# Sums of weights in a Strassen-form up-projection: two of four made by an adding transfer, the others by VectorE

## The chip, the cores and the metric

The kernel runs on one core of one Trainium2 chip. The metric is the device time of one execution in microseconds (us), as the median of several runs.

## The reference

The kernel computes two layers of a decoder trunk, for one sequence of 512 tokens and a model width of 1024, in float32. Each layer is a half-step feed-forward network (FFN), a token mixer with three branches, and a second FFN, each conditioned on a vector c. The FFN is where the change lies:

```python
def swiglu(h, w_up, w_down):
    gate, up = jnp.split(h @ w_up, 2, axis=-1)
    return (jax.nn.silu(gate) * up) @ w_down

def reference(x, c, ...):
    for l in range(DEPTH):
        mod = (jnp.einsum('bd,de->be', jax.nn.silu(c), w_ada[l]) + b_ada[l]).reshape(b, 9, d)
        h = modulate(rmsnorm(x, norm_g[l, 0]), mod[:, 0], mod[:, 1])
        x = x + 0.5 * mod[:, 2][:, None] * swiglu(h, w_ffn_in[l, 0], w_ffn_out[l, 0])
        ...
        x = x + mod[:, 5][:, None] * y
        h = modulate(rmsnorm(x, norm_g[l, 2]), mod[:, 6], mod[:, 7])
        x = x + 0.5 * mod[:, 8][:, None] * swiglu(h, w_ffn_in[l, 1], w_ffn_out[l, 1])
    return x
```

D_FF is 2816, so `h @ w_up` is a product of 512x1024 by 1024x5632.

## The kernel before

The six sub-layers are called by their number n from 1 to 6: n = 1, 3, 4 and 6 are FFNs, n = 2 and 5 the mixers. Every float32 operand is split into a high and a low part of type float32r, and every product is three matmuls (high by high, high by low, low by high). For a block of weights `weight` (L254) hands out the pair, `halves` (L219) makes it: ScalarE copies the block into the high part (`wh`, L224), VectorE subtracts that from the block for the low part (`wl`, L228). Blocks are prepared two ahead of their use (`AHEAD = 2`).

Most of the up-projection is done in a form of Strassen's method with seven products where eight would be needed, and four sums on either side. The activations are cut in four quarters (tiles `hq`) and `sums` (L544) makes the four sums of them once at the start of each such stage and splits each (`sh` on ScalarE, `sl` on VectorE at L267). The weights come in pairs of column blocks j; each pair has four quarter blocks 11, 21, 12, 22 of 128x1024 (512 KB). `block` (L231) loads the four on SyncE's DMA queue (SP) into tiles `wr` and makes four sums on VectorE: t1 = 12 - 11 (L244, into a tile `t`), t2 = 22 - t1 (L246, a second tile `t`), 22 - 12 in place of 12 (L248), and 21 - t2 in place of 21 (L251). The products of a pair run in the order 1, 2, 6, 7, 5, then 1 of the next pair, 3, 4; product 1 takes block 11, 2 takes 21, 6 takes t2, 7 takes 22 - 12, 5 takes t1, 3 takes 22 and 4 takes 21 - t2. Each product is 24 matmuls of 128x128 by 128x256 (L582). There are 39 such pairs: 9 in n = 1 and 10 in each of n = 3, 4 and 6. `pair` (L585) adds the products' banks up (L607, L613) and makes silu(gate) * up; columns outside the pairs go through `finish` (L641).

Buffers and queues order the work around this. Raw blocks rotate through 5 buffers, `wh` and `wl` through 3 each. The tiles `t`, the quarters `hq` and the rows `ada` of the conditioning (loads of 512 KB at L428, used by VectorE at L429) share one tag `z` of 4 buffers (`z4k`, L119), so at a stage's start a tile of one kind gets its buffer when a quarter has been read for the last time, by its `sl` split. A scheduler fixes each engine's order of instructions when the program is built. SP issues in its order and waits at an instruction whose buffer isn't free. Conditioning work goes on beside n = 1, 3 and 4, not beside n = 6.

Of the kernel before, what the change touches and what calls it, by code (L numbers as in the profile page):

```python
# [17 lines left out]
ALU = mybir.AluOpType  # L18
# [55 lines left out]
class Trunk:  # L74
# [156 lines left out]
    def block(self, l, f, j, p):  # L231


        sub = self.nc.vector.tensor_tensor
        if p == 1:
            self.pairs[j] = {}
            for q in (11, 21, 12, 22):
                t = self.raw()
                self.nc.sync.dma_start(t, self.io["w_up"][l, f, j, (11, 21, 12, 22).index(q)])
                self.pairs[j][q] = t  # L240
        b = self.pairs[j]
        if p == 6:
            b["t1"] = self.z4k("t")
            sub(b["t1"], b[12], b[11], op=ALU.subtract)  # L244
            b["t2"] = self.z4k("t")
            sub(b["t2"], b[22], b["t1"], op=ALU.subtract)  # L246
        elif p == 7:
            sub(b[12], b[22], b[12], op=ALU.subtract)  # L248
        elif p == 4:

            sub(b[21], b[21], b["t2"], op=ALU.subtract)  # L251
        return b[{1: 11, 2: 21, 6: "t2", 7: 12, 5: "t1", 3: 22, 4: 21}[p]]

    def weight(self, *key):  # L254
        while len(self.loaded) < AHEAD:
# [176 lines left out]
    def ada_done(self, l, s, kind, ks=(0, KD)):  # L432
        nc = self.nc
        a, b = ks
        m0 = (3 * s + kind) * 8
        m = self.mod[l][:, m0 + a:m0 + b]
        o = slice(8 * s + a, 8 * s + b)
        bias = self.p(l, PO_BADA + m0 + a, b - a)
        if kind == 0:
            nc.vector.tensor_tensor(self.shift[l][:, o], m, bias, op=ALU.add)  # L440
        elif kind == 1:
            nc.vector.tensor_tensor(m, m, bias, op=ALU.add)
            nc.vector.scalar_tensor_tensor(self.amp[l][:, o], m, 1.0,
                                           self.p(l, PO_NORM + 8 * s + a, b - a),
                                           op0=ALU.add, op1=ALU.mult)
        else:
            nc.vector.tensor_tensor(self.res[l][:, o], m, bias, op=ALU.add)
            if s != 1:
                nc.vector.tensor_scalar(self.res[l][:, o], self.res[l][:, o], 0.5, None, op0=ALU.mult)

    def ada_jobs(self, l, kinds):
        jobs = []
# [91 lines left out]
    def sums(self):  # L544

        tt = self.nc.vector.tensor_tensor
        a11, a12, a21, a22 = (self.quarters[q] for q in (11, 12, 21, 22))
        self.S = {}

        def keep(n, t):  # L550
            self.S[n] = (self.t4k([P, D], F32R, "sh"), self.t4k([P, D], F32R, "sl"))
            self.split(self.S[n], t)

        tt(a22, a21, a22, op=ALU.add)
        tt(a21, a11, a21, op=ALU.subtract)
        tt(a11, a22, a11, op=ALU.subtract)
        keep(2, a11)
        keep(3, a21)
        keep(1, a22)
        tt(a12, a12, a11, op=ALU.subtract)  # L560
        keep(4, a12)
        self.quarters = {}

# [19 lines left out]
                                     stop=(k, x) == (3, 2), skip_group_check=True)  # L583

    def pair(self, l, f, j, st, nxt, acts):  # L585


        nc = self.nc
        tt = nc.vector.tensor_tensor

        def run(st, j, p, tag, first=True):
            if first:
                st[p] = self.bank(tag)
            self.product(l, f, j, p, st[p], first)

        def snap(name):
            st[name] = self.t2k(name)
            nc.scalar.activation(st[name], st[1], AF.Copy)  # L598

        def more(p):  # L600
            self.product(l, f, j, p, st[1], False)

        if 1 not in st:
            run(st, j, 1, "mm")
        snap("c11")
        run(st, j, 2, "s")
        tt(st["c11"], st["c11"], st[2], op=ALU.add)  # L607
        more(6)
        snap("u2")
        run(st, j, 7, "s")  # L610
        more(5)
        snap("c22")
        tt(st["c22"], st["c22"], st[7], op=ALU.add)  # L613
        later = {}
        if nxt is not None:
            run(later, nxt, 1, "mm")
        more(3)
        self.product(l, f, j, 4, st[7], False)
        act = self.t4k([P, 2, T], F32, "act")
        halves = [act[:, :, h] for h in HALF]  # L620

        def two(t):
            return t.rearrange("p (a b) -> p a b", a=2)

        nc.scalar.activation(st["c11"], st["c11"], AF.Silu)
        tt(halves[0], two(st["c11"]), two(st[1]), op=ALU.mult)
        tt(st["u2"], st["u2"], st[7], op=ALU.add)
        nc.scalar.activation(st["u2"], st["u2"], AF.Silu)
        tt(halves[1], two(st["u2"]), two(st["c22"]), op=ALU.mult)
        hi, lo = self.act_tiles("a")  # L630
        self.split((hi, lo), act)
        for i in range(2):
            acts[2 * j + i] = (hi[:, i, :], lo[:, i, :])
        return later

    def ffn(self, n, l, f, ada, cb, stats, nxt, first=None):
        nc, io = self.nc, self.io
        s = 2 * f
        acts = {}

        def finish(m, pg, pu):  # L641
            sl = self.t2k("sil")
            nc.scalar.activation(sl, pg, AF.Silu)
            nc.vector.tensor_tensor(sl, sl, pu, op=ALU.mult)
            acts[m] = self.act_pair("a")
            self.split(acts[m], sl)

        def unit(g):
            return lambda d: self.weight("down", l, f, g, d)

        def more(k):
            for _ in range(k):
                if ada:
                    ada.popleft()(cb)

        if first:
            banks = [self.bank(t) for t in ("mm", "mm", "mm", "mm", "s", "s")]
            for k in range(KD):
                w = first(k)
                for j in range(6):  # L660
                    self.mm(banks[j], w, slice(j * P, (j + 1) * P), self.h[k], k == 0, k == KD - 1)
            for m in range(3):
                finish(m, banks[2 * m], banks[2 * m + 1])
            self.sums()
            self.ready = True
        early = []
        blocks = self.ffn_blocks(n)
        st = {}
        for (kind, i), after in zip(blocks, blocks[1:] + [("end", 0)]):
            if kind == "plain":  # L670
                if i == 0:
                    early = self.head(lambda j: self.weight("in", l, f, j // 2, j % 2))
                    self.sums()
                ps = []
                for j in range(2):
                    if early:
                        ps.append(early.pop(0))
                        continue
                    w = self.weight("in", l, f, i, j)
                    ps.append(self.bank("mm"))  # L680
                    self.mmk(ps[j], w, self.h, range(KD), 0, KD - 1)
                finish(i, ps[0], ps[1])
                more(2)
            elif kind == "pair":
                st = self.pair(l, f, i, st, after[1] if after[0] == "pair" else None, acts)
                more(2)
            else:
                a, b = GROUPS[i]
                for d in range(KD):
                    w = unit(i)(d)  # L690
                    ps = self.bank("mm")
                    self.mmk(ps, w, acts, range(a, b), a, b - 1, base=a)
                    self.residual(l, s, d, ps, FULL, None)
                    more(2)
        more(len(ada or ()))
        self.tail(l, s, unit(2), acts, GROUPS[2], GROUPS[2][0], stats, nxt)
# [529 lines left out]
```

## Time and profile before

| | |
|---|---|
| median of 3 runs | 2660.65 us (2656.46, 2660.65, 2661.26) |
| profiled execution, its own time | 2660.07 us |
| its span | 2658.3 us |
| TensorE (PE) busy | 2519.4 us, 95% of the span |
| VectorE (DVE) busy | 2005.5 us, 75% |
| ScalarE (ACT) busy | 1126.6 us, 42% |
| GpSimd (POOL) busy | 337.7 us, 13% |
| mean granted TensorE clock | 0.977 of full speed |
| moved by DMA | 312.22 MB, mean 117 GB/s |

A busy time is the sum over an engine's instructions; where the engines work side by side, only the one that others wait for sets the time. Waits are listed by the engine that waited, its line, and what released it. Product rows carry the tile names: a matmul into `mm` or `s` is a product into a PSUM bank, `hh` and `hl` are the split activations, `sh` and `sl` the split sums of them.

### The profile page before, as it was taken

The page shows a single profiled execution, that of the slowest core. Times are in us where ns is not written, and L with a number is a line of the kernel's source. Part 1 is how long each engine was busy: PE and PEld are TensorE (multiplying, and loading weights), DVE is VectorE, ACT ScalarE, POOL GpSimd, SP SyncE. Part 2 cuts the span into 40 slices and gives each one's busy share as a digit, 9 for nine tenths or more (in the row PEclk, how much of TensorE's full clock was granted, in tenths as well). Part 3 has the DMA queues.
Part 4 walks back from the last instruction along what each step waited for, and adds up shares of the span by engine and source line. Part 5 has one row for each costly group of instructions (what it writes and reads, how often), then busy time and mean ns, then how long its engine had stood idle before and what let it go on. Part 6 is the DMA issues. An engine that isn't in the chain of part 4 may idle for free.

```text
span 2658.3 us, 38054 instructions
## 1 busy us (share of the span) xinstructions
PE 2519.4 (95%) x15072; PEld 2211.8 (83%) x15072; DVE 2005.5 (75%) x3383; ACT 1126.6 (42%) x1765; POOL 337.7 (13%) x289
## 2 busy tenths in 40 slices
PE   7999999699999998999989999977999999999999
PEld 5989888578877888898979898866787788898988
DVE  8989879987864469986689885699878634785855
ACT  4525342245562345343455353423556423553523
POOL 2000004980000000000000000069600000000000
PEclk9999999799999999999999999988999999999999
DMA  7465644212223324735335632321221332233332
GB/s 265 156 225 189 216 140 122 63 58 64 72 85 97 93 75 161 270 117 166 104 104 195 215 118 79 100 68 56 64 72 52 95 95 88 72 104 95 104 95 88
DMA packets 97749, 312.22 MB, mean 117 GB/s; under 512 B 10345, under 2 KB 17257, under 8 KB 97570
## 3 DMA queue, kind: packets, MB, share of 16 engines
q1 hardware_dynamic: 97424, 309.65, 36.7%
q8 instruction: 118, 1.93, 0.3%
q14 instruction: 61, 0.50, 0.1%
q10 hardware_dynamic: 146, 0.14, 0.0%
HBM read 307.62 MB, written 6.06 MB: 118 GB/s over the span
## 4 chain that ended last, share of the span: by engine, by line
PE 81%; DVE 14%; ACT 2%; issue 2%; DMA 1%; DVEq 0%; ACTq 0%
PE mm L582 17%; PE mm L272 13%; PE mm L276 13%; PE mm L274 13%; PE s L582 12%; DVE ca L756 3%; PE mm L822 2%; PE mm L826 2%; PE mm L824 2%; DVE wl L228 2%; PE s L885 2%; PE o L954 1%; DVE ada L429 1%; PE s L927 1%; DMA ada<-in_w_ada 1%
## 5 line engine op out<-in xcount | busy, mean ns | idle before, releaser
L224 ACT ACTIVATE wh<-wr 128x1024 fp32r<-128x1024 f32 (+1 forms) x481 | 485.5, 1010 | 689.6 <-PE mm L276 326.9
L228 DVE TENSOR_TENSOR wl<-wr,wh 128x1024 fp32r<-128x1024 f32 (+1 forms) x468 | 557.2, 1192 | 236.2 <-ACT wh L224 234.5
L272 PE MATMUL mm<-ah,wh 128*128 128x512 f32 (+1 forms) x752 | 287.2, 383 | 0.0
L276 PE MATMUL mm<-al,wh 128*128 128x512 f32 (+1 forms) x752 | 286.8, 382 | 0.0
L274 PE MATMUL mm<-hh,wl 128*128 128x512 f32 (+1 forms) x776 | 281.8, 366 | 5.2 <-DVE wl L228 5.1
L274 PE MATMUL mm<-ah,wl 128*128 128x512 f32 (+1 forms) x752 | 286.3, 382 | 0.0
L272 PE MATMUL mm<-hh,wh 128*128 128x512 f32 (+1 forms) x776 | 281.5, 366 | 2.8 <-ACT hh L491 2.7
L276 PE MATMUL mm<-hl,wh 128*128 128x512 f32 (+1 forms) x776 | 276.4, 367 | 5.6 <-DVE hl L498 5.3
L582 PE MATMUL mm<-sh,wh 128*128 128x256 f32 x936 | 267.5, 286 | 10.5 <-ACT c L598 8.2
L582 PE MATMUL mm<-sh,wl 128*128 128x256 f32 x936 | 266.4, 285 | 1.1 <-DVE wl L228 1.1
L582 PE MATMUL mm<-sl,wh 128*128 128x256 f32 x936 | 266.0, 284 | 0.0
L822 PE MATMUL mm<-wh,hh 128*128 128x384 f32 x512 | 189.6, 370 | 34.4 <-DVE v L832 21.5
L507 DVE SCALAR_TENSOR_TENSOR x<-mm,res,x 128x512 f32<-128x512 f32 (+1 forms) x124 | 86.1, 697 | 175.3 <-PE mm L276 175.3
L582 PEld LDWEIGHTS mm<-sh,wh 128*128 128x128 f32 x936 | 180.3, 193 | 13.6 <-ACT c L598 10.7
L824 PE MATMUL mm<-wl,hh 128*128 128x384 f32 x512 | 187.8, 367 | 0.0
L582 PE MATMUL s<-hh,wl 128*128 128x256 f32 x624 | 174.9, 280 | 12.6 <-DVE wl L228 12.6
L826 PE MATMUL mm<-wh,hl 128*128 128x384 f32 x512 | 185.5, 362 | 0.0
L582 PEld LDWEIGHTS mm<-sh,wl 128*128 128x128 f32 x936 | 180.6, 193 | 1.7 <-DVE wl L228 1.7
L582 PEld LDWEIGHTS mm<-sl,wh 128*128 128x128 f32 x936 | 180.8, 193 | 0.0
L429 DVE SCALAR_TENSOR_TENSOR ada<-ada,cb 128x1024 f32<-128x1024 f32 x144 | 174.6, 1226 | 4.4 <-DMA ada<-in_w_ada 4.3
L582 PE MATMUL s<-hl,wh 128*128 128x256 f32 x624 | 176.1, 282 | 0.0
L582 PE MATMUL s<-hh,wh 128*128 128x256 f32 x624 | 175.6, 281 | 0.0
(218 smaller groups left out, 5900.9 us busy)
## 6 DMA issues: line engine op xcount, KB each, us to landing
wr<-in_w_up SPq DMA_DIRECT2D x156, 512.0 KB, 3.7
ada<-in_w_ada SPq DMA_DIRECT2D x144, 512.0 KB, 5.4
wr<-in_w_down SPq DMA_DIRECT2D x64, 512.0 KB, 4.8
wr<-in_w_qkv SPq DMA_DIRECT2D x64, 384.0 KB, 3.2
wr<-in_w_gate SPq DMA_DIRECT2D x48, 512.0 KB, 3.6
wr<-in_w_down SPq DMA_DIRECT2D x32, 384.0 KB, 3.1
wr<-in_w_branch SPq DMA_DIRECT2D x24, 512.0 KB, 3.6
wr<-in_w_u SPq DMA_DIRECT2D x16, 512.0 KB, 3.6
```

The costliest lines, as they stand in the source:

```text
L224: nc.scalar.activation(hi[:, :n], raw[:, :n], AF.Copy)
L228: eng.tensor_tensor(lo[:, :n], raw[:, :n], hi[:, :n].bitcast(F32), op=ALU.subtract)
L272: nc.tensor.matmul(ps[:, rng], w[0][:, wcol], ah[:, rng], start=start, stop=False)
L274: nc.tensor.matmul(ps[:, rng], w[1][:, wcol], ah[:, rng], start=False, stop=False)
L276: nc.tensor.matmul(ps[:, rng], w[0][:, wcol], al[:, rng], start=False, stop=stop)
L429: nc.vector.scalar_tensor_tensor(w, w, 1.0, cb, op0=ALU.mult, op1=ALU.mult, accum_out=self.mod[l][:, e:e + 1])
L507: self.nc.vector.scalar_tensor_tensor(self.x[d][:, rng], ps[:, rng], self.res[l][:, 8 * s + d:8 * s + d + 1], self.x[d][:, rng], op0=ALU.m ...
L582: nc.tensor.matmul(o, w[a][:, c], acts[k][b], start=first and (mi, k, x) == (0, 0, 0), stop=(k, x) == (3, 2), skip_group_check=True)
L756: eng.scalar_tensor_tensor(ca[j], u, w, ca[j], op0=ALU.mult, op1=ALU.add)
L822: nc.tensor.matmul(o, hi[:, hs], w[0][:, ws], start=k == 0, stop=False)
L824: nc.tensor.matmul(o, hi[:, hs], w[1][:, ws], start=False, stop=False)
L826: nc.tensor.matmul(o, lo[:, hs], w[0][:, ws], start=False, stop=k == KD - 1)
```

## The change

The signs of the scheme are turned so that t1 is 11 + 12 and the block of product 7, now called t3, is 12 + 22: plain sums. Each of the two is made by a load of its first quarter on SP (L243) followed by a second transfer of the other quarter from HBM, issued by GpSimd, that adds into the same tile (L245, `accum_op`). Block 12 is no longer loaded alone; t1 takes its `z` buffer when the pair is begun (p == 1) and not at product 6, and t3 takes a raw buffer. VectorE makes t2 = 22 + t1 (L249) and 21 + t2 (L251). On the other side of the products, two sums of activations in `sums` become one `scalar_tensor_tensor` each in place of a `tensor_tensor`, so does the product in `finish` (with a factor -1), and the factor 0.5 of the residual becomes -0.5.

```diff
--- before.py
+++ after.py
@@ -231,25 +231,25 @@
     def block(self, l, f, j, p):
 
 
-        sub = self.nc.vector.tensor_tensor
+
+        add = self.nc.vector.tensor_tensor
+        dma = self.nc.sync.dma_start
         if p == 1:
-            self.pairs[j] = {}
-            for q in (11, 21, 12, 22):
-                t = self.raw()
-                self.nc.sync.dma_start(t, self.io["w_up"][l, f, j, (11, 21, 12, 22).index(q)])
-                self.pairs[j][q] = t
+            self.pairs[j] = b = {}
+            src = {q: self.io["w_up"][l, f, j, i] for i, q in enumerate((11, 21, 12, 22))}
+            for name, q, more in ((11, 11, None), ("t1", 11, 12), (21, 21, None), (22, 22, None),
+                                  ("t3", 12, 22)):
+                b[name] = self.z4k("t") if name == "t1" else self.raw()
+                dma(b[name], src[q])
+                if more:
+                    self.nc.gpsimd.dma_start(b[name], src[more], accum_op=ALU.add)
         b = self.pairs[j]
         if p == 6:
-            b["t1"] = self.z4k("t")
-            sub(b["t1"], b[12], b[11], op=ALU.subtract)
             b["t2"] = self.z4k("t")
-            sub(b["t2"], b[22], b["t1"], op=ALU.subtract)
-        elif p == 7:
-            sub(b[12], b[22], b[12], op=ALU.subtract)
+            add(b["t2"], b[22], b["t1"], op=ALU.add)
         elif p == 4:
-
-            sub(b[21], b[21], b["t2"], op=ALU.subtract)
-        return b[{1: 11, 2: 21, 6: "t2", 7: 12, 5: "t1", 3: 22, 4: 21}[p]]
+            add(b[21], b[21], b["t2"], op=ALU.add)
+        return b[{1: 11, 2: 21, 6: "t2", 7: "t3", 5: "t1", 3: 22, 4: 21}[p]]
 
     def weight(self, *key):
         while len(self.loaded) < AHEAD:
@@ -446,7 +446,7 @@
         else:
             nc.vector.tensor_tensor(self.res[l][:, o], m, bias, op=ALU.add)
             if s != 1:
-                nc.vector.tensor_scalar(self.res[l][:, o], self.res[l][:, o], 0.5, None, op0=ALU.mult)
+                nc.vector.tensor_scalar(self.res[l][:, o], self.res[l][:, o], -0.5, None, op0=ALU.mult)
 
     def ada_jobs(self, l, kinds):
         jobs = []
@@ -551,13 +551,15 @@
             self.S[n] = (self.t4k([P, D], F32R, "sh"), self.t4k([P, D], F32R, "sl"))
             self.split(self.S[n], t)
 
-        tt(a22, a21, a22, op=ALU.add)
+        less = self.nc.vector.scalar_tensor_tensor
+
+        tt(a22, a22, a21, op=ALU.subtract)
         tt(a21, a11, a21, op=ALU.subtract)
-        tt(a11, a22, a11, op=ALU.subtract)
+        less(a11, a22, -1.0, a11, op0=ALU.mult, op1=ALU.subtract)
         keep(2, a11)
         keep(3, a21)
         keep(1, a22)
-        tt(a12, a12, a11, op=ALU.subtract)
+        less(a12, a12, -1.0, a11, op0=ALU.mult, op1=ALU.subtract)
         keep(4, a12)
         self.quarters = {}
 
@@ -583,6 +585,7 @@
                                      stop=(k, x) == (3, 2), skip_group_check=True)
 
     def pair(self, l, f, j, st, nxt, acts):
+
 
 
         nc = self.nc
@@ -641,7 +644,8 @@
         def finish(m, pg, pu):
             sl = self.t2k("sil")
             nc.scalar.activation(sl, pg, AF.Silu)
-            nc.vector.tensor_tensor(sl, sl, pu, op=ALU.mult)
+
+            nc.vector.scalar_tensor_tensor(sl, sl, -1.0, pu, op0=ALU.mult, op1=ALU.mult)
             acts[m] = self.act_pair("a")
             self.split(acts[m], sl)
```

The instruction order on VectorE at the start of n = 6, before. Here wr_3432, 3433, 3434, 3435 are the blocks 11, 21, 12, 22 of the first pair, t_3445 is t1 and t_3446 is t2; wl_3442 is for product 2, wl_3448 for 6, wl_3450 for 7, wl_3454 for 5:

```order
L267 TENSOR_TENSOR al_3431_21451<-sil_3429_21447,ah_3430_21450 128x512
L644 TENSOR_TENSOR sil_3439_21491<-sil_3439_21491,mm_3438_21466 128x512
L228 TENSOR_TENSOR wl_3442_21498<-wr_3433_21456,wh_3441_21497 128x1024
L267 TENSOR_TENSOR al_3431_21451<-sil_3439_21491,ah_3430_21450 128x512
L244 TENSOR_TENSOR t_3445_21528<-wr_3434_21458,wr_3432_21454 128x1024
L246 TENSOR_TENSOR t_3446_21530<-wr_3435_21460,t_3445_21528 128x1024
L607 TENSOR_TENSOR c11_3443_21525<-c11_3443_21525,s_3444_21527 128x512
L248 TENSOR_TENSOR wr_3434_21458<-wr_3435_21460,wr_3434_21458 128x1024
L228 TENSOR_TENSOR wl_3448_21533<-t_3446_21530,wh_3447_21532 128x1024
L251 TENSOR_TENSOR wr_3433_21456<-wr_3433_21456,t_3446_21530 128x1024
L228 TENSOR_TENSOR wl_3450_21563<-wr_3434_21458,wh_3449_21562 128x1024
L228 TENSOR_TENSOR wl_3454_21594<-t_3445_21528,wh_3453_21593 128x1024
```

The same stretch in the changed kernel, where wr_3434 is block 21, wr_3435 is 22, wr_3436 is t3, t_3433 is t1 and t_3446 is t2; wl_3443 is for product 2, wl_3448 for 6, wl_3450 for 7, wl_3454 for 5:

```order
L267 TENSOR_TENSOR al_3431_21480<-sil_3429_21476,ah_3430_21479 128x512
L648 SCALAR_TENSOR_TENSOR sil_3440_21524<-sil_3440_21524,mm_3439_21499 128x512
L228 TENSOR_TENSOR wl_3443_21531<-wr_3434_21488,wh_3442_21530 128x1024
L267 TENSOR_TENSOR al_3431_21480<-sil_3440_21524,ah_3430_21479 128x512
L249 TENSOR_TENSOR t_3446_21561<-wr_3435_21490,t_3433_21485 128x1024
L251 TENSOR_TENSOR wr_3434_21488<-wr_3434_21488,t_3446_21561 128x1024
L228 TENSOR_TENSOR wl_3448_21564<-t_3446_21561,wh_3447_21563 128x1024
L610 TENSOR_TENSOR c11_3444_21558<-c11_3444_21558,s_3445_21560 128x512
L228 TENSOR_TENSOR wl_3450_21593<-wr_3436_21492,wh_3449_21592 128x1024
L228 TENSOR_TENSOR wl_3454_21624<-t_3433_21485,wh_3453_21623 128x1024
```

The rows of L244 and L248 are gone; L249 takes the place of L246 and reads a tile that only transfers have written, and L251 now stands ahead of the split for product 6. At the starts of n = 3 and n = 4 the three rows L249, L251 and that split follow each other in the same way; at n = 1 one row L429 stands between L249 and L251.

SP's queue at the start of n = 6, before: the four blocks of the first pair, then those of the second:

```order
L239 DMA wr_3432_21454<-in_w_up 128x1024
L239 DMA wr_3433_21456<-in_w_up 128x1024
L239 DMA wr_3434_21458<-in_w_up 128x1024
L239 DMA wr_3435_21460<-in_w_up 128x1024
L239 DMA wr_3455_21621<-in_w_up 128x1024
L239 DMA wr_3456_21623<-in_w_up 128x1024
L239 DMA wr_3457_21625<-in_w_up 128x1024
L239 DMA wr_3458_21627<-in_w_up 128x1024
```

SP's queue there in the changed kernel:

```order
L243 DMA wr_3432_21483<-in_w_up 128x1024
L243 DMA wr_3434_21488<-in_w_up 128x1024
L243 DMA wr_3435_21490<-in_w_up 128x1024
L243 DMA wr_3436_21492<-in_w_up 128x1024
L243 DMA wr_3455_21651<-in_w_up 128x1024
L243 DMA wr_3457_21656<-in_w_up 128x1024
L243 DMA t_3433_21485<-in_w_up 128x1024
L243 DMA t_3456_21653<-in_w_up 128x1024
L243 DMA wr_3458_21658<-in_w_up 128x1024
L243 DMA t_3485_21885<-in_w_up 128x1024
```

The first four rows are blocks 11, 21, 22 and the first half of t3 (wr_3436). The first half of t1 (t_3433) stands after two blocks of the second pair, since its `z` buffer comes free only when the first `sl` split of the stage has ended. At n = 1 it likewise waits for the first `sl` split; at n = 3 and 4 it stands behind two rows `ada` and waits for the third.

GpSimd's queue there in the changed kernel (the row of L228 is the last one that stood there before too):

```order
L228 TENSOR_TENSOR wl_3411_21294<-wr_3409_21291,wh_3410_21293 128x1024
L245 DMA wr_3436_21492<-in_w_up 128x1024
L245 DMA t_3433_21485<-in_w_up 128x1024
L245 DMA t_3456_21653<-in_w_up 128x1024
L245 DMA t_3485_21885<-in_w_up 128x1024
L245 DMA wr_3459_21660<-in_w_up 128x1024
L245 DMA t_3514_22117<-in_w_up 128x1024
L245 DMA wr_3488_21892<-in_w_up 128x1024
```

The adding transfers are in the order t3 of the first pair, t1 of the first, second and third pair, then t3 of the second; each waits for its own first half, and what stands behind it waits with it.

## Rows read from the trace of the kernel before

**Rows 1.** Page, part 1: busy us of each engine (share of the span) and its instructions.

```profile
PE 2519.4 (95%) x15072; PEld 2211.8 (83%) x15072; DVE 2005.5 (75%) x3383; ACT 1126.6 (42%) x1765; POOL 337.7 (13%) x289
```

**Rows 2.** Chain of waits in n = 3: start us, length us, what.

```profile
1025.81 8.59 PE mm L582 x72
...
1045.81 8.59 PE mm L582 x72
```

**Rows 3.** Waits of PE: line, releaser: us in all, times, longest us.

```profile
PE s L582 <- DVE wl L228: 12.6, 3, 8.4
PE mm L582 <- ACT c L598: 8.2, 12, 0.7
PE mm L582 <- DVE wl L228: 7.7, 4, 6.5
```

**Rows 4.** Tile t: instructions, ns least/median/most, first and last start.

```profile
L244 DVE TENSOR_TENSOR t<-wr,wr x39: 1211/1218/1227, 81.0 to 2589.6; 128x1024 f32<-128x1024 f32 x39
L246 DVE TENSOR_TENSOR t<-wr,t x39: 1218/1225/1229, 82.2 to 2595.4; 128x1024 f32<-128x1024 f32 x39
```

**Rows 5.** Waits of DVE, columns as in rows 3.

```profile
DVE t L246 <- DMA wr<-in_w_up: 31.5, 29, 2.4
...
DVE t L244 <- DMA wr<-in_w_up: 14.0, 12, 1.6
```

**Rows 6.** DMA issues: times, KB each, median us from issue to landing.

```profile
wr<-in_w_up SPq DMA_DIRECT2D x156, 512.0 KB, 3.7
ada<-in_w_ada SPq DMA_DIRECT2D x144, 512.0 KB, 5.4
...
bias<-rvec SPq DMA_DIRECT2D x12, 320.0 KB, 10.0
```

**Rows 7.** Windows: us, busy PE PEld DVE ACT POOL, PE clock, DMA share, GB/s.

```profile
88.00:90.00 2.00, 2.00 (x11) 2.00 (x11) 2.00 (x3) 0.00 (x0) 0.00 (x0) 0.52 0.79 145
...
1018.00:1020.00 2.00, 1.31 (x10) 1.11 (x8) 2.00 (x3) 1.72 (x2) 0.00 (x0) 0.91 1.02 404
...
1400.00:1500.00 100.00, 99.31 (x686) 92.08 (x686) 96.39 (x122) 43.05 (x49) 0.00 (x0) 1.00 0.69 237
...
2332.00:2336.00 4.00, 3.51 (x16) 3.51 (x17) 3.83 (x4) 1.39 (x2) 0.00 (x0) 0.57 0.04 6
```

**Rows 8.** Timelines of SP, DVE and PE, start of n = 1: start us, length, instruction [idle before].

```profile
71.47 1.46 SPq L428 DMA_DIRECT2D ada<-in_w_ada  x2
...
79.83 1.22 DVE L228 TENSOR_TENSOR wl<-wr,wh 128x1024 fp32r<-128x1024 f32 x1
...
86.37 0.47 PE L582 MATMUL mm<-sh,wl 128*128 128x256 f32 x1 [0.20 <-DVE wl L228]
```

**Rows 9.** Timelines of DVE and PE, start of n = 3.

```profile
1001.13 4.62 DVE L267 TENSOR_TENSOR sl<-hq,sh 128x1024 fp32r<-128x1024 f32 x4
...
1012.97 1.22 DVE L228 TENSOR_TENSOR wl<-wr,wh 128x1024 fp32r<-128x1024 f32 x1
...
1014.24 0.58 PE L582 MATMUL s<-hh,wl 128*128 128x256 f32 x1 [8.38 <-DVE wl L228]
...
1020.04 0.38 PE L582 MATMUL mm<-sh,wl 128*128 128x256 f32 x1 [0.73 <-DVE wl L228]
```

**Rows 10.** Timelines of DVE and PE, start of n = 4.

```profile
1369.55 4.75 DVE L267 TENSOR_TENSOR sl<-hq,sh 128x1024 fp32r<-128x1024 f32 x4
...
1383.58 1.22 DVE L244 TENSOR_TENSOR t<-wr,wr 128x1024 f32<-128x1024 f32 x1
...
1388.98 0.39 PE L582 MATMUL mm<-sh,wl 128*128 128x256 f32 x1 [0.20 <-DVE wl L228]
```

**Rows 11.** Timelines of DVE and PE, start of n = 6.

```profile
2319.46 4.62 DVE L267 TENSOR_TENSOR sl<-hq,sh 128x1024 fp32r<-128x1024 f32 x4
...
2326.94 1.22 DVE L244 TENSOR_TENSOR t<-wr,wr 128x1024 f32<-128x1024 f32 x1
...
2332.87 0.41 PE L582 MATMUL mm<-sh,wl 128*128 128x256 f32 x1
```

## Prediction

> **What bounds the kernel now.** The first view is the page's busy times [rows 1]: the matmul engine is busy 95% of the span, VectorE 75%. That average decides nothing, so the second is the chain of waits in the middle of a stage of pairs [rows 2]: it runs through matmuls alone, and the same piece returns after 20.0 us (1025.81, 1045.81, and so on). Product by product that is 8.59 / 3 = 2.86 us. Inside these stages PE waits for nobody. The third view is the list of PE's waits [rows 3]: for the low halves of the pairs' blocks PE waited 12.6 + 7.7 us in seven waits; the longest, 8.4, is at the start of n = 3 [rows 9], the next, 6.5, at that of n = 4. The 8.2 us for `c` are twelve short waits for a PSUM bank, which no instruction of the change frees. So of 2660 us about 20 can be reached by making weight sums sooner, and only at four stage starts. There VectorE runs one instruction after another (L267, L429, L228, L244 and so on), and product 6 starts in full about 1.27 us after the start of its `wl`: 1014.24 - 1012.97 for product 2 in n = 3 [rows 9].
>
> One profiled execution gives all durations. It took 2660.07 us for a span of 2658.3, and is 0.6 us under the median of the three runs shown; my sums start from 2660.07.
>
> **VectorE's part, inside the stages.** The change takes away 39 instructions at L244 and 39 at L248; L246 and L251 stay under new numbers, each still a 128x1024 sum of 1.22 us [rows 4]. Started back to back, instructions of this size step by some 1.14 us (four `sl` take 4.62: (4.62 - 1.22) / 3, rows 11), so 78 x 1.14 = 89 us of VectorE's work go. I cost this at zero: the matmuls of rows 2 cover it, and they wait for nothing there. Were that cover gone, it would be worth 2 x 1.14 us a pair. Also at zero: two sums per stage and the product in `finish` in another form of the same size, and the factor -0.5.
>
> **The transfers' part, inside the stages.** SP issues five loads per pair in place of four: block 11 is read a second time for t1, and block 12 becomes the first half of t3. GpSimd issues two adding transfers per pair, 78 in all, that were not there. Three blocks of 524 kB more per pair leave HBM, 61 MB in all. In the densest stretch the queues moved 237 GB/s at a share of 0.69 [rows 7]; three blocks in 20 us are 79 GB/s more, and 52 on top if the old contents are read too, together 368 of the 404 GB/s that a short window reached [rows 7]. It fits, not by much. As to lateness: the first half of t3 is issued when the raw buffer comes free, five products (14.3 us) and VectorE's lead of some 3 us before the split for product 7, so first half and adding transfer may take some 17 us together, and with 5.4 for the first [rows 6] the adding one has some 11.5. t2 still waits for block 22 as L246 did: that wait was 31.5 us in 29 times, with 14.0 more at L244 [rows 5], and none of it reached PE inside a stage. So far no change.
>
> **The starts.** Here the change acts. Before, product 6 came after L244, L246 and, at some starts, L248 or L251, on a VectorE that had hardly a gap. Now it waits for t1: its first half can be issued only when an `sl` split has freed a buffer, must land, and then the adding transfer runs, before L249 can. Let X be the time from the landing of the first half to the landing of the sum, and A the start of L249. By the order L251 and the split follow, so product 6 starts at A + 2 x 1.14 + 1.27, that is A + 3.56; at n = 1 one L429 more, A + 4.70.
> - n = 1: VectorE is ready at 79.83 (one L429 of 1.14 has moved behind; the `wl` of rows 8 starts at 78.69). The first half is issued at 71.47, where the rows `ada` were [rows 8], and lands 3.7 later [rows 6]: A is the later of 79.83 and 75.3 + X, to be set against 86.37.
> - n = 3: two L429 now stand behind the split for product 2, so product 2 starts at 1011.4 in place of 1014.24. VectorE is ready at 1013.5: 1012.97 + 1.14, less 0.6 for the `finish` product (128x512), which now fills a wait for `ada` ahead of these. The first half follows the third `sl` (1001.13 + 3 x 1.14 = 1004.6, rows 9) and two loads `ada`, 5.4 with them: A is the later of 1013.5 and 1010.0 + X; before: 1020.04 [rows 9].
> - n = 4: A is the later of 1383.58, where L244 stood, and 1373.1 + 5.4 + X; before: 1388.98 [rows 10].
> - n = 6: the first half follows the first `sl` (2320.6) and lands 3.7 later: A is the later of 2326.94 and 2324.35 + X; before: 2332.87 [rows 11].
>
> **X is the unknown.** No row of before shows an adding transfer, nor any transfer of such a size that GpSimd issued. From below: a plain load of the same 512 KB, 3.7 [rows 6]. From above: two such loads' worth, 7.4, or the slowest transfer in the list, 10.0 for 320 KB in pieces [rows 6]. The nearest row is the plain load: of its 3.7, 524 kB / 404 GB/s = 1.3 are moving and 2.4 are fixed. With the old contents read as well that is 5.0 alone, and 6.7 from the 5.4 that a block takes among others. I take 6.0, an estimate. Then n = 1 gains 86.37 - 86.0 = 0.4, n = 3 0.5, n = 4 0.9, and n = 6 loses 1.0: +0.8 in sum. In n = 3 product 2 ends at some 1016.5 and PE then idles 3 us, which may cost clock again: in the windows at 0.52 and 0.57 [rows 7], right behind such waits at n = 1 and n = 6, (1 - 0.52) x 2 = 1.0 and (1 - 0.57) x 4 = 1.7 us were lost, so I take off 1.5. Net 0.7 slower: **2661 us**.
>
> The plain load's 3.7 us is what the trace has. The Trainium skill (DMA: Bandwidth & Descriptors, Anatomy of one DMA) fits a transfer issued from GpSimd with 2.0 us and the bytes at 436 GB/s, an estimate of 3.2 us for this size, and by that the sum would be that of the first rival. No row of this case shows one.
>
> **Rivals.**
> - *The adding transfer is as quick as a plain load,* X = 3.7. Then VectorE's own order decides nearly everywhere: n = 1 gains 1.8, n = 3 2.8, n = 4 1.8, n = 6 1.3 (A = 2328.05), 7.7 in all, and the half clock after the waits at n = 1 and n = 6 [rows 7] need not come, 2.7: 2660.07 - 10.4 = 2649.7. For it: bytes and HBM side are those of rows 6. Against: it must read what it adds to. It beats 0.2% (5.3 us, about what a measurement of this kernel can tell from no change) from X below some 4.8.
> - *The adding transfer is slow,* X = 9, since GpSimd has to write its orders while VectorE is busy without gaps, or since the queues are full at the starts (a share of 1.02 from 1018 to 1020) [rows 7]. Product 6 then starts late at all four: -2.6, -2.5, -2.1, -4.0, and 1.5 of clock: 2660.07 + 12.7 = 2673. It decides from X = 5.8 on, where the four and the clock sum to zero; each us more costs 4. Over 0.2% it needs X above some 7.1. The Trainium skill (SBUF — State Buffer, Who interferes with whom) says that GpSimd can be kept from writing descriptors by VectorE instructions that take both ports, and that `tensor_tensor` is not one of them; no run here shows either.
> - *The adding transfer is so slow that every pair waits,* X above 11.5 to 12: then the split for product 7 comes late in some 35 pairs, 1 us each for each us over; X = 13 gives 2660 + 4 x 7.2 = 2689 from the starts and 35 x 1.25 = 44 from the pairs, some 2733.
> - *The change does not do what it says:* excluded by the order of the instructions, which shows the 78 sums gone and 78 adding transfers in.
>
> **How the numbers follow.** X below 4.8: 0.22; 4.8 to 7.1: 0.42; 7.1 to 11.5: 0.28; above: 0.08. So faster 0.22, within 0.2% 0.42, slower 0.36. The range runs from X = 3.7 (2650) to X = 9.5 (2675), which leaves out the quickest few and the pairs' stall. The middle case alone spans 2656 to 2666.
>
> **What would show it.** From a landing of a first half of t1 to L249's start there should be about 6 us at the four starts, with L249 waiting for a DMA there; pairs should still repeat every 20.0 us; VectorE should be busy some 90 us less. Wrong would be: L249 starting at VectorE's own pace (X small), a period over 20.0 us or PE waiting for `wl` in the middle of a stage (X large), or PE waiting for a bank that ScalarE or VectorE frees later in the new order.

## The result: 48 us slower, most of it inside the pairs

The changed kernel takes 2709.47 us (median of 4 runs, 2708.76 to 2712.87) against 2660.95 us for the kernel before (4 runs): a ratio of 1.0183, 95% interval 1.0167 to 1.0200. That is 48.5 us slower; the forecast was 2661 and the range ended at 2675. Times are of executions at a granted TensorE clock of 0.97 to 0.99; one of e10, at 0.745, took 3074 us and is left out.

The busy times and the DMA queues on the page of the changed kernel (q1 carries SP's loads, q0 what GpSimd issues: packets, MB, share of 16 engines' time):

```profile
span 2707.6 us, 38318 instructions
...
PE 2536.8 (94%) x15072; PEld 2218.9 (82%) x15072; DVE 1923.8 (71%) x3305; ACT 1119.9 (41%) x1765; POOL 404.9 (15%) x367
...
q1 hardware_dynamic: 103040, 330.10, 37.4%
q0 software_dynamic: 11232, 40.90, 8.8%
```

VectorE is busy 81.7 us less than in [rows 1], as the change promised, and nothing came of it. q0 moved 40.90 MB in 8.8% of the span, q1 eight times as much in 37.4%: 172 GB/s against 326 GB/s while their packets ran. A byte that is added takes about twice as much of the queues' time as one that is loaded.

The waits of PE, of the pairs' products alone, beside [rows 3]:

```profile
PE s L584 <- DVE wl L228: 19.6, 16, 5.9
PE mm L584 <- DVE wl L228: 18.0, 16, 6.4
PE mm L584 <- ACT wh L224: 8.8, 4, 2.6
PE s L584 <- ACT wh L224: 8.2, 12, 1.2
```

Before, low halves were waited for seven times, at stage starts; now 32 times. And VectorE's own waits for DMA, beside [rows 5], with the one for `ada` before as the last row:

```profile
DVE ada L429 <- DMA ada<-in_w_ada: 80.6, 41, 6.7
DVE t L249 <- DMA wr<-in_w_up: 25.2, 24, 2.6
DVE t L249 <- DMA t<-in_w_up: 12.3, 4, 4.0
```

```profile
DVE ada L429 <- DMA ada<-in_w_ada: 4.3, 7, 1.6
```

The wait for block 22 at L249 has not grown. The four waits for t1 are the four stage starts. New are 80.6 us for the conditioning loads `ada`, 4.3 us before.

Where the 48 us lie follows from the first matmul of each product. The first pair of each stage is longer by 2.7, 1.2, 1.2 and 1.8 us (n = 1, 3, 4, 6), 6.9 in all. The other pairs are longer by 13.7, 12.0, 11.7 and 4.3 us, 41.7 in all. In n = 3, say, pairs that took 20.00 us take 21.3 and 22.9. PE's busy time grew by 17.4 us too (2536.8 against 2519.4). Matmuls of 0.28 us follow each other every 0.12; where a wait breaks them, the last runs out its 0.16 alone and the first after it is recorded with 0.38, some 0.26 us of busy time a break. And 126 matmuls took over 390 ns, not 69. They lie where the granted clock is at the lower of its two levels, 1.2 of 2.4 GHz (0.50 from 1490 to 1493), right behind waits: no longer once at each stage start alone, but a second time early in n = 3 and in n = 6 and once inside n = 4 (near 1490). At some 0.1 us each that is 6 us.

The chain of waits in n = 3 shows what repeats (start us, length us, what):

```profile
1067.54 5.35 DMA wr<-in_w_up
...
1073.59 8.34 DMA wr<-in_w_up
...
1082.04 1.06 ACT wh L224
...
1083.13 1.24 DVE wl L228
...
1084.38 3.56 DMA wr<-in_w_up
...
1088.03 0.09 DVE t L249
...
1089.17 1.23 DVE wl L228
...
1090.42 5.09 DMA wr<-in_w_up
```

The rows are: first half of t3; its adding transfer; the split for product 7, which frees t3's raw buffer; the load of the next block 22 into that buffer; t2, which waits for it; behind it on VectorE the split for the next product 1, which frees the buffer that the next t3 takes; and again the first half of t3. The loop closes after 1090.42 - 1067.54 = 22.88 us, where matmuls need 20.0 [rows 2]. Without the time from the first half's landing (1072.89) to that of the sum (1081.94) it is 13.83 us, so X, the time between these two landings that the prediction left open, may be 6.2 at most here. It was 9.05. The row of t2 in VectorE's timeline shows that the loop is nearly as long without block 22:

```profile
1088.03 1.23 DVE L249 TENSOR_TENSOR t<-wr,t 128x1024 f32<-128x1024 f32 x1 [0.21 <-DMA wr<-in_w_up]
```

t2 waited for the block for 0.21 us. Until then VectorE worked through what stands behind the late split for product 7 in its fixed order.

The landings of the adding transfers at L245, and GpSimd's own part, from the view of that line (ns least/median/most):

```profile
L245 POOL DMA_DIRECT2D t<-in_w_up x39: 856/865/882, 76.1 to 2609.2; - x39
...
DMA to landing us min/median/max: 5.3/7.0/10.3
```

### The profile page after: what moved, and what is told of

Read it like the earlier page. It is cut to its first block, busy times and chain, and to the rows that moved or that the text cites. A ratio compares the mean times of both kernels' runs of the same rounds, so it can differ in the third digit from the quotient of the medians.

```text
span 2707.6 us, 38318 instructions
## 1 busy us (share of the span) xinstructions
PE 2536.8 (94%) x15072; PEld 2218.9 (82%) x15072; DVE 1923.8 (71%) x3305; ACT 1119.9 (41%) x1765; POOL 404.9 (15%) x367
## 3 DMA queue, kind: packets, MB, share of 16 engines
q1 hardware_dynamic: 103040, 330.10, 37.4%
q0 software_dynamic: 11232, 40.90, 8.8%
q8 instruction: 118, 1.93, 0.3%
## 4 chain that ended last, share of the span: by engine, by line
PE 65%; DVE 17%; DMA 11%; issue 3%; ACT 3%; SPq 0%; POOLq 0%; DVEq 0%; ACTq 0%
PE mm L272 13%; PE mm L276 13%; PE mm L274 13%; PE mm L584 8%; DMA wr<-in_w_up 6%; PE s L584 6%; DVE wl L228 4%; DMA ada<-in_w_ada 3%; DVE ca L760 3%; PE mm L826 2%; PE mm L830 2%; PE mm L828 2%; PE s L889 2%; DVE ada L429 2%; DMA t<-in_w_up 2%
## 5 line engine op out<-in xcount | busy, mean ns | idle before, releaser
L228 DVE TENSOR_TENSOR wl<-wr,wh 128x1024 fp32r<-128x1024 f32 (+1 forms) x468 | 556.5, 1193 | 295.2 <-ACT wh L224 294.1
L429 DVE SCALAR_TENSOR_TENSOR ada<-ada,cb 128x1024 f32<-128x1024 f32 x144 | 174.3, 1220 | 80.7 <-DMA ada<-in_w_ada 80.6
L826 PE MATMUL mm<-wh,hh 128*128 128x384 f32 x512 | 188.8, 369 | 34.6 <-DVE v L836 21.6
```

Source lines behind the costliest of these rows:

```text
L228: eng.tensor_tensor(lo[:, :n], raw[:, :n], hi[:, :n].bitcast(F32), op=ALU.subtract)
L429: nc.vector.scalar_tensor_tensor(w, w, 1.0, cb, op0=ALU.mult, op1=ALU.mult, accum_out=self.mod[l][:, e:e + 1])
L826: nc.tensor.matmul(o, hi[:, hs], w[0][:, ws], start=k == 0, stop=False)
```

## The experiments

Seventeen kernels ran. "Before" is the kernel before in the same session (2660 to 2661.5 us). The edits are abridged; `-` is the changed kernel, `+` the run, unless it is said otherwise. Lengths of single pairs and waits are those of the one profiled execution of each run.

**The signs alone.**

```diff
-  t1: load 11 (SP) + add 12 (GpSimd);  t3: load 12 + add 22
+  t1 = 12 + 11, t3 = 22 + 12 in place of 12, both on VectorE; loads 11, 21, 12, 22
```

> The signs as in the change, but all four sums of weights on VectorE as before (39 more sums for t1, 39 more for t3), four plain loads per pair, no adding transfer. Theory (the transfers and the buffers they hold cost the time): as before, 2660 within 5 us, pairs 20.0 us. Rival (the turned signs, other instruction forms or the new order cost something of their own): 2670 or more.

Measured 2659.96 us, ratio 0.9998 (0.9988 to 1.0007). Signs and instruction forms cost nothing; all of the loss is in the transfers.

**One of the two transfers at a time.** In e2 only t1 is made by transfer:

```diff
-  ("t3", 12, 22)      # load and adding transfer
+  (12, 12, None)      # plain load, ahead of 22; at p == 7: add(b[12], b[22], b[12]) on VectorE
```

> Only t1 by load and adding transfer; block 12 is loaded plainly and VectorE makes t3 in its place. Theory (two separate costs: t3's adding transfer closes a loop through the raw buffers, t1's early claim of a z buffer starves the conditioning loads): no wait for product 7's low half, but VectorE still waits 50 us or more for ada loads in all, stalls in n = 1, 3 and 4 and none inside n = 6; 2680 to 2690. Rival (only the loop of t3 costs): starts aside 2660, so 2662 to 2668. Rival (only the traffic of adding transfers costs): half of the loss, 2685, in n = 6 as well.

Measured 2671.81, ratio 1.0041 (1.0026 to 1.0056). The first pairs are longer by 3.1, 3.3, 3.4 and 3.0 us, and the others lose 0.7 us in all: the loss lies at the starts. VectorE does wait for ada (37.1 us), but PE doesn't notice. So t1's transfer alone costs what the slow rival had for the starts, and no pair. In e9 only t3 is:

```diff
-  ("t1", 11, 12)      # load and adding transfer
+  ("t1", 12, None)    # plain load; at p == 6: add(b["t1"], b["t1"], b[11]) on VectorE
```

> The complement of e2: t3 by load and adding transfer in the place it has in the change; the tile of t1 is filled by a plain load of block 12 and VectorE adds block 11 to it at product 6. Five loads and one adding transfer per pair. Theory (the adding transfer of t3 sits in a loop through five raw buffers, by itself enough for the stalls): waits for product 7 or for t2 inside the pairs of n = 1, 3 and 4, 2680 to 2700. Rival (it takes t1's adding transfer as well, through the queues and the z buffers): pairs of 20.0 us, 2658 to 2668.

Measured 2675.66, ratio 1.0056 (1.0040 to 1.0071): less than expected. Pairs stall, but only some (21.4 and 22.0 us in n = 3 and 4, most 20.0; where a down-projection stands between two pairs, up to 69.6 us in place of 65.9). The two alone add up to 11 + 14 us, together they cost 48: they do not simply add. t3's landings are not longer beside t1's transfers: 6.0 us at the median in the change, 7.5 in e9.

**Other places in the loop.** In e3 t3 stands ahead of 22 in the list of loads:

```diff
-  (21, 21, None), (22, 22, None), ("t3", 12, 22)
+  (21, 21, None), ("t3", 12, 22), (22, 22, None)
```

> The change with the load and adding transfer of t3 put ahead of the load of block 22, so that t3 takes over the raw buffer of the t3 before it, not that of the next block 11. Theory (loop load of t3, adding transfer, split for product 7, load of 22, t2, split for product 1, load of t3 lasts 22.9 us): product 7 no longer waits inside a stage, 20 us or so come back, 2685 to 2695. Rival (the adding transfers are slow wherever they stand): 2705 to 2712.

Measured 2699.25, ratio 1.0142 (1.0126 to 1.0159). Product 7 no longer waits, but t2's wait for block 22 grew from 25.2 to 104.5 us, since 22 now takes the late buffer; pairs of 21.4 to 24.7 us remain. With buffers this short, a new order hands the wait on. In e8 t2 = 11 + t3 and t1 = t2 - 22, with one adding transfer a pair:

```diff
-  t1 by transfer; t2 = 22 + t1
+  t2 = 11 + t3 (VectorE, p == 6); t1 = t2 - 22 (VectorE, p == 5)
```

> Only t3 by load and adding transfer, from its place ahead of block 22; VectorE makes t2 = 11 + t3, t1 = t2 - 22 and 21 + t2, and block 12 isn't loaded alone: four loads and one adding transfer per pair. Theory (what costs at the starts is t1's late buffer, what costs in the pairs is the loop in which t1 and t3 both wait for 22 and each other): the first t3 of a stage is made before the stage begins, so L249 starts at VectorE's own pace, product 6 comes 1 to 2 us earlier than before at the four starts; pairs 20.0 us: 2650 to 2660. Rival (any adding transfer into a raw buffer closes the loop): product 6 or 7 waits inside the pairs of n = 1, 3, 4, 2675 to 2695.

Measured 2712.09, ratio 1.0196 (1.0181 to 1.0211). Each theory has half: the first pairs, up to the start of product 4, were *shorter* than before by 3.2, 1.0, 1.9 and 3.0 us, but t2 waited 146.3 us for t3 in the other pairs, in n = 6 too.

**What makes the transfer slow.** In e7 the second transfer copies:

```diff
-  self.nc.gpsimd.dma_start(b[name], src[more], accum_op=ALU.add)
+  self.nc.gpsimd.dma_start(b[name], src[more])
```

> The change with the second transfers of t1 and t3 issued by GpSimd as before, but as plain copies (the sums of weights are left out: the second block overwrites the first). Theory (adding makes a transfer slow, since it moves about twice the data): from issue to landing 3.5 to 4.5 us in place of 6.0 to 7.2, the loop falls below 20 us, few stalls inside stages, 2663 to 2675. Rival (issuing from GpSimd, or the third more bytes, is what is slow): landings of 6 us and more, 2695 or more.

Measured 2662.38, ratio 1.0012 (1.0003 to 1.0022). Same queue, same order, same bytes from HBM; the kernel leaves out the sums. The page's row for q0 and the view of L245:

```profile
q0 software_dynamic: 11232, 40.90, 4.6%
```

```profile
L245 POOL DMA_DIRECT2D t<-in_w_up x39: 527/527/533, 75.5 to 2560.2; - x39
...
DMA to landing us min/median/max: 3.8/4.8/8.2
```

The same 40.90 MB took 4.6% of the queues, not 8.8%, and landed 2.2 us sooner at the median (0.34 of it GpSimd's own part), and nearly all pairs take 20.0 us again. Where the trace tells both landings (26 of 39 pairs), X of t3 was 5.8 us at the median (4.3 to 8.9); in the change it was 7.6 (5.9 to 10.8). So single passes of the loop were still too long, but not one after the other. That GpSimd issues the transfer and that 61 MB more are moved is not the cause, the adding is. The Trainium skill (Collectives: The Full Stack, The bandwidth ceiling) says that an add in the DMA path has to read two sources, and measures a factor of 1.93 between a collective that copies (AllGather) and one that adds (ReduceScatter). Here it is 8.8 / 4.6 = 1.9 for a transfer of one core, and the trace agrees with the factor; the reads themselves it does not show.

**Memory for the loops.** e5 gives a sixth raw buffer, its room taken from the split activations:

```diff
-  tag="wraw", bufs=5;  tags "ah", "al", bufs=5
+  tag="wraw", bufs=6;  tags "ah", "al", bufs=4
```

> The change with 6 raw buffers in place of 5 (4 KB of room, taken from the split activations: 4 buffers each for their high and low parts in place of 5). Theory (a loop through the raw buffers makes the pairs' stalls): no waits for product 7 inside a stage, pairs of 20.0 us in n = 1, 3 and 4, and what is left is the loss at the four starts, about the 11 us that t1's adding transfer alone cost: 2668 to 2678. Rival (the traffic of adding transfers delays everything, buffers or not): 2695 or more.

> The kernel before with 4 buffers each for the split activations in place of 5: what the room for the sixth raw buffer costs by itself. Both theories: 2660 to 2664.

The room itself is free: e6 took 2660.44 us, ratio 1.0000 (0.9989 to 1.0010). But e5 took 2719.94, ratio 1.0225 (1.0209 to 1.0240), far from the theory's time. The rival has the time, but not the place: in n = 6, where no conditioning loads run, all pairs fell to 20.0 us, as the loop through raw buffers wants. In the other stages a second loop showed: VectorE waited 109.0 us for ada. That wait, and its chain in n = 3:

```profile
DVE ada L429 <- DMA ada<-in_w_ada: 109.0, 52, 5.7
```

```profile
1206.82 1.14 DVE wl L228
...
1207.98 6.74 DMA ada<-in_w_ada
...
1214.82 0.17 DVE ada L429
...
1216.08 4.24 DMA ada<-in_w_ada
```

A `z` buffer comes free when t1's split ends; the conditioning load issued in that moment lands 6.74 us later, and VectorE, whose order is fixed, stands at L429 until then; that frees the buffer for the next. t1 holds one of four `z` buffers through a load and an adding transfer. With six raw buffers and t3 alone (e10):

```diff
   (e9, with the buffers of e5)
```

> e9 with a sixth raw buffer (room as in e5, which cost nothing in e6). Theory (the loop goes through the raw buffers): all pairs 20.0 us, 2652 to 2662. Rival (the adding transfer is late wherever its buffer comes from): as e9, 2680 or more.

Measured 2689.88 (three runs, 2681.11 to 2699.22), ratio 1.0110 (1.0085 to 1.0136); VectorE's waits for ada went from 21.6 us in e9 to 48.8. But its waits for raw blocks at the sum of t1 grew as well, from 22.8 to 52.7 us, and pairs of n = 6 took up to 21.5 us, where no conditioning loads run. The second loop does not explain that; why e10 is slower than e9 stays open.

**What the second loop is not.** e4 holds t1's buffer as early, without any adding:

```diff
-  ("t1", 11, 12)      # load and adding transfer;   ("t3", 12, 22)
+  ("t1", 11, None)    # at p == 6: add(b["t1"], b["t1"], b[12]);   t3 on VectorE
```

> No adding transfer: the z buffer of t1 is claimed at the pair's begin by a plain load of block 11, and VectorE adds 12 to it at product 6, as it makes t3, t2 and the last sum. Theory (t1's early claim starves the conditioning loads of z buffers): VectorE waits 40 us or more for ada loads (4.3 before), pairs of n = 1, 3, 4 stall, n = 6 doesn't; 2672 to 2688. Rival (the adding transfers themselves are the cost): 2660 within 5 us and few waits for ada.

Measured 2661.54, ratio 1.0004 (0.9995 to 1.0013), 6.4 us of waits for ada: an early claim costs nothing while the tile is quick to fill. e11 cuts the bytes of the conditioning loads, and VectorE's work on them, to a quarter:

```diff
-  nc.sync.dma_start(w, self.io["w_ada"][l, e])
+  nc.sync.dma_start(w[:, :256], self.io["w_ada"][l, e][:, :256])
```

> The change with the conditioning loads beside the FFN stages cut to a quarter of their columns, and their products on VectorE too (three quarters of that sum are left out). Theory (what closes the loops in n = 1, 3 and 4 is that ada loads and adding transfers lengthen each other): pairs of n = 1, 3 and 4 behave as those of n = 6 in the change, 20.0 us but for one or two before a group of w_down loads; adding transfers land in some 5.5 us at the median; 2672 to 2688. Rival (the loops close without ada loads): 2695 or more.

Measured 2706.13, ratio 1.0171 (1.0152 to 1.0189), with 88.4 us of waits for ada: their bytes are not it. e13 takes the first halves of t1 and t3 off SP's queue, e14 adds the sixth raw buffer:

```diff
-  dma(b[name], src[q])
+  (self.nc.gpsimd.dma_start if more else dma)(b[name], src[q])
```

> The change with the first halves of t1 and t3 issued by GpSimd too, ahead of their adding transfers; SP issues blocks 11, 21, 22 and the conditioning loads alone. Theory (two orders hold the pairs: the loop of t3 through five raw buffers, and SP's queue, in which ada loads stand behind first halves that wait for buffers held by adding transfers, with VectorE waiting in its own order for ada): VectorE's waits for ada fall from 80.6 us to 20 or less, product 7's waits stay, 2685 to 2700. Rival (ada loads are late for lack of z buffers, not for their place in SP's queue): waits for ada of 50 us and more, 2705 or more.

> e13 with the sixth raw buffer of e5. Theory (both causes taken away): pairs of 20.0 us in all four stages but for one or two, and the loss at the starts, 2668 to 2680. Rival (z buffers): the waits for ada grow as in e5, 2700 or more.

Measured 2724.96, ratio 1.0243 (1.0226 to 1.0260), and 2733.35, ratio 1.0279 (1.0263 to 1.0294). VectorE waited 79.8 and 131.1 us for ada. So a place behind first halves in SP's queue is not needed for these waits; the rival, `z` buffers, stands. The test is not a clean one: in e13 and e14 each first half stands in GpSimd's queue behind adding transfers, which wait there for their own first halves (38 and 14 waits, 134.7 and 74.8 us in e13).

**Both loops opened.** e16 has a fifth `z` buffer, e17 a fifth `z` and a sixth raw one:

```diff
-  tag="z", bufs=4;  tag="wraw", bufs=5
+  tag="z", bufs=5;  tag="wraw", bufs=5 (e16), 6 (e17)
```

> The change with 5 z buffers in place of 4 (room from the split activations as in e5), 5 raw buffers. Theory (two loops of the same kind, one through the raw buffers by way of t3, one through the z buffers by way of t1 and the conditioning loads): VectorE's waits for ada fall from 80.6 us to 25 or less, product 7's waits in the pairs stay: 2685 to 2700. Rival (z buffers are not short; the traffic of the adding transfers delays ada): ada waits of 60 us and more, 2705 or more.

> The change with 5 z and 6 raw buffers (room from the split activations and from one of five buffers of each of the small tiles). Theory (the two loops, both opened): pairs of 20.0 us in all stages but for a few, the loss at the four starts stays: 2666 to 2680. Rival (opening one only moves the wait on): 2695 or more.

Measured 2688.40, ratio 1.0101 (1.0084 to 1.0118), and 2661.13, ratio 1.0004 (0.9995 to 1.0013). In e16 waits for ada fell to 52.3 us, not to 25, and product 7's waits stayed. In e17 the waits of PE and VectorE are as follows; the last row is that of e16:

```profile
PE mm L584 <- DVE wl L228: 13.3, 7, 5.8
PE s L584 <- DVE wl L228: 9.2, 5, 2.3
```

```profile
DVE ada L429 <- DMA ada<-in_w_ada: 57.7, 30, 5.1
```

```profile
DVE ada L429 <- DMA ada<-in_w_ada: 52.3, 26, 5.2
```

VectorE waits as long as in e16, but now has the slack: low halves hold PE up 12 times, not 32. The adding transfers are as slow as ever (medians 6.3 and 7.1 us). The other pairs still cost some 15 us more than before. The first pairs give that back: they are shorter by 3.2, 0.2, 8.0 and 3.5 us, though at n = 4 the first pair also begins 5.3 us later behind n = 3. At n = 1 the reason is that t1's first half, with a buffer more, need not wait for an `sl` split: it is issued at 41.44 us, not 71.88, and L249 no longer waits. So two buffers of 4 KB per partition bring the change back to the time of the kernel before. They do not show that the transfers are then free: the kernel before was not run with these two buffers, and might have gained at the starts too. Nor was the further room that e17 takes (from the small tiles) tried by itself.

**A version that beats both.** Since e8 won at the starts, e12 uses its sums there alone:

```diff
+  first = j == (2 if (l, f) == (0, 0) else 1)
+  if first: t3 = load 12 + add 22 by GpSimd;  t2 = 11 + t3;  t1 = t2 - 22
   other pairs: as e1
```

> An adding transfer for t3 of the first pair of each stage alone, issued before the stage begins; there t2 = 11 + t3 and t1 = t2 - 22 on VectorE. All other pairs as in e1, on VectorE. Theory (only the four starts have anything to win, and there a sum that is ready early saves VectorE two instructions ahead of product 6): product 6 comes 1 to 3 us earlier at each start, pairs 20.0 us: 2648 to 2655. Rival (what is won at the start is given back behind it): 2659 to 2662.

Measured 2650.92 us, ratio 0.9963 (0.9951 to 0.9976): some 10 us faster than the kernel before. The first pairs are shorter by 3.2, 1.1, 1.6 and 3.3 us, and all others take what they took. e15 takes its last four adding transfers away:

```diff
-  if first: t3 = load 12 + add 22 by GpSimd
+  if first: t3 = 12 + 22 on VectorE, in place of 12
```

> e12 without any transfer that adds: in the first pair of each stage VectorE makes t3 = 12 + 22 in place, t2 = 11 + t3 and t1 = t2 - 22, so that one of its sums moves behind product 6. Theory (what e12 won is two sums less ahead of product 6, half of it by the order of the sums): 2654 to 2658. Rival (all of it is the order of the sums): 2650 to 2652. Rival (all of it is the transfer): 2659 to 2662.

Measured 2652.71, ratio 0.9972 (0.9960 to 0.9983). That is some 8 us of the 10, so most of the gain is the order of the sums; the intervals of e12 and e15 overlap, and whether the four transfers bring the rest is not shown. The timeline of VectorE in e15 at n = 6, against [rows 11]; the last row is the split for product 6 before:

```profile
2304.62 1.22 DVE L246 TENSOR_TENSOR wr<-wr,wr 128x1024 f32<-128x1024 f32 x1
...
2321.76 1.22 DVE L248 TENSOR_TENSOR t<-wr,wr 128x1024 f32<-128x1024 f32 x1
...
2324.17 1.23 DVE L228 TENSOR_TENSOR wl<-t,wh 128x1024 fp32r<-128x1024 f32 x1
```

```profile
2331.21 1.22 DVE L228 TENSOR_TENSOR wl<-t,wh 128x1024 fp32r<-128x1024 f32 x1
```

t3 needs no `z` buffer, so VectorE makes it 17 us ahead; then t2 is the first thing it does where L244 stood before. From there to the end of the split for product 6 it takes 2325.40 - 2321.76 = 3.64 us, before 2332.43 - 2326.94 = 5.49: its low half is one or two sums nearer. The first matmul of product 6, which needs the high half alone, comes no sooner (0.4 us later at n = 6); product 7 starts 1.9, 0.05, 1.5 and 2.9 us sooner behind product 1 (n = 1, 3, 4, 6).

## Why the prediction was wrong

**What held.** The pairs were bound by PE, and the 81.7 us taken off VectorE were worth nothing. t2's wait for block 22 stayed as it was (25.2 us). The signs and the other forms cost nothing (e1). L249 waits for t1 at each of the four starts, for the reason given.

**The size of X.** I took 6.0 us, between 5.0 alone and 6.7 among others. At n = 3 it was 6.2 (first half landed at 1026.5, sum at 1032.8), at n = 6 6.2, at n = 1 8.5 and at n = 4 8.6. The starts cost 6.9 us where my sum had a gain of 0.8 before the clock. By itself that would have been 2668, inside the range. With these X in place of 6.0 the prediction's own sums for the starts give a loss of 4.8 us, and 6.3 with its 1.5 for the clock, near the 6.9 measured. The working, "with the old contents read as well", fits e7 in kind, and its 1.3 us was near: by the rows of q0 an adding transfer keeps the queues busy for 8.8% x 2707.6 / 78 = 3.1 us, a copy for 4.6% x 2658.5 / 78 = 1.6. Left out were the 0.6 us from the first half's landing to GpSimd's order (1026.54 to 1027.10 at n = 3), GpSimd's own 0.87 us, and that landings spread as they do, 5.3 to 10.3 us.

**The step that failed** is the one on lateness inside the stages: "first half and adding transfer may take some 17 us together", so "the adding one has some 11.5". It followed t3 once, from the release of its buffer to its use. I costed the wait of t2 for block 22 on its own, as unchanged. In fact the two are links of one loop: the buffer that 22 waits for is the one that t3 has just left, and the buffer for the next t3 comes free behind t2 on VectorE, which comes to t2 only behind the late split for product 7. A lead covers one late pass; a delay in a loop returns each pair. The right question was whether the loop's lengths add up to less than 20.0 us on average, and in the pass shown that leaves 6.2 us for X, not 11.5. For t3, e7 lies below that at the median (5.8), the change above (7.6). In n = 6 of the change X was 5.9 to 6.9 us in six of the seven pairs whose landings the trace tells, and most pairs there took 20.0 us.

**The step that was missing** is `z`. I counted a buffer's release for t1 at the starts alone. Inside n = 1, 3 and 4, t1, t2 and the conditioning loads share four buffers, and t1 now holds one for a load and an adding transfer before anything reads it. That is the second loop; e5 (2720 us), e16 (2688) and e17 (2661) show that both had to be opened.

**The rivals.** "So slow that every pair waits" was the right mechanism, with a bound of 11.5 to 12 that should have been about 6, and with a chance of 0.08 that hung on that bound. "GpSimd is kept from writing its orders" did not come up: its part is 0.86 to 1.02 us each time (0.53 for a copy).

What is not settled: how much of the longer landings, 5.3 us at best and 10.3 at worst, comes from conditioning loads and how much from the two adding transfers meeting each other. e11 lowered the median for t3 only from 6.0 to 5.9, and e9, with one adding transfer a pair, has 7.5. Nor is it settled what the 52 to 58 us of waits for ada come from that stay with a fifth `z` buffer (e16, e17).

## To carry to other kernels

When a step with longer latency goes into a pipeline with few buffers, follow each buffer round until it comes back to the same step, through the engines' fixed orders, and add up the lengths: on average the sum must stay below the period, and a lead that covers a single late pass does not change that. Work moved off an engine that nobody waits for is worth nothing; the same sums in an order that lets the first of them run before the stage begins were worth 8 us. Where a loop is just too long, one more buffer in one of two loops can make things worse (2720 us in e5) or only partly better (2688 in e16); one in both can make them whole (2661 us in e17).

## What was unexpected of the hardware

An adding transfer of 512 KB from HBM took 1.9 times the queue time of a copy of the same bytes from the same queue (8.8% against 4.6% of the span) and landed in 5.3 us at best against 3.8, with 0.87 us of GpSimd's time at the median against 0.53. The Trainium skill (DMA: Bandwidth & Descriptors, Anatomy of one DMA) fits 3.2 us, an estimate, for a transfer of this size; the copies took at least 3.8, and adding is not in that fit.
